# One more attention head in the seven-product form, a closer timetable, and moved buffers in a fused decoder layer

## The chip, the cores and the metric

The kernel runs on one core of a Trainium2 chip. The metric is the device time of one execution in microseconds (us), as the median of several runs. The core's engines work side by side, each through its own instruction queue in order: PE (TensorE, matrix products), DVE (VectorE), ACT (ScalarE), POOL (GpSimd) and SP (which here only issues transfers). PEld is PE's loading of weights. Matrix products are collected in PSUM, eight banks of 128 x 512 float32.

## The reference

One decoder layer on 512 tokens of width 2048 in float32. The part that the change is in is the token mixer:

```
h = rmsnorm(x, attn_pre_norm)
proj = h @ w_in                       # 2048 x 6160
gq, gk, gv, gg, ga, dq, dk, dv = ...  # column ranges of proj
...
o_a = gla_chunked(gq, gk, gv, log_a)                 # 4 heads, 128 keys, 256 values
o_a = rmsnorm(o_a, gla_norm) * silu(gg)
o_b = diff_attention(dq, dk, dv, lam)                # 4 heads, two softmaxes each
o_b = rmsnorm(o_b, diff_norm) * (1.0 - lambda_init)
m = concat(o_a, o_b) @ w_o
x = x + rmsnorm(m, attn_post_norm)
```

A gated MLP of width 5632 with a causal convolution follows; the change does not touch it.

## The kernel before

Every float32 operand of a large product is split into a high and a low part (`whi`, `wlo` for weights by `granule`, L116; `ah`, `al` for the activations), and a product is three matmuls: high by high, high by low, low by high. Weights come in granules of 128 x 1024 numbers (512 KB): ACT makes the high part, DVE the low one.

The stages are these. `first_half` loads x, normalizes and transposes it into `ah` and `al`, and begins the first 512 columns of gv. Set-up work stands behind it in the code (L474 to L530): masks, `keep`, the lambda sums, the columns of the convolution. Then the rest of gv, the forget gate's input (`forget_in`, with the small operand `gas`), and the sums for the next form (`mixer_sums`: `s5`, `s2`, `s3`).

Next come the units. A `Unit` (L209) computes 512 columns as two blocks of 256 with seven products of half size in place of eight (Strassen's scheme): fourteen granules, each 24 matmuls of 128x256 (`up_prods`, L318 to L320, or `token_prods`, L329 to L331). Sums of weight blocks are made by DMAs with addition on the POOL queue (`more`, L228) and by DVE. Units stand for gq and gk (two), the second half of gv, dv (two), and the first STRASSEN_HEADS heads of dq and dk. Their results go to DRAM and come back as rows when the attention wants them. `p1` (in `mix_unit.copy`) is a copy of the first product that a unit keeps until its last one.

The attention stage runs on a timetable. `gran` is a list of plain granules, each 24 matmuls of 128x512, in four parts; a part and what the timetable lays beside it make a tick. In the list stand dq and dk of the heads that are not units (`plan_t`, L162 to L164), the two halves of the gate gg (`plan_n`, L181 to L183, with `gate` at the end of each bank), and seven granules of w_o. `END` is the tick at which w_o begins. `spawn(gen, at)` puts a generator on tick `at`; each `yield n` sends it n ticks on. GLA_EVERY is the distance of the levels of a GLA head (`gla_head`, seven `gla_level`, `gla_tail`), BLOCK_EVERY that of the 16 `query_block`s, STATE_EVERY that of the four chunks in a `gla_tail`. `gated_row` multiplies GLA rows with gate rows and transposes them, `reload` brings a head of the differential attention back. Inside this stage the order on PE, ACT, DVE and POOL is that of the code; what waits, waits in its queue, and all behind it too. The attention's products take their PSUM banks from a ring of four (`psa`), the plain granules from another of four (`psm`).

The activation's lower left quarter is overwritten during the units and comes back from DRAM on the POOL queue in front of the last `y2`; the plain granules start with the half that was not overwritten.

Of the kernel before, what the change touches and what calls it, by code (L numbers as in the profile page):

```python
# [9 lines left out]
F32 = mybir.dt.float32  # L10
# [3 lines left out]
ALU = mybir.AluOpType  # L14
# [3 lines left out]
P = 128  # L18
D = 2048
S = 512  # L20
# [3 lines left out]
GH, GDK, GDV, RANK = 4, 128, 256, 16  # L24
TAU = 16.0
DH, DQK, DDV = 4, 128, 256
# [3 lines left out]
C_GQ, C_GK, C_GV, C_GG, C_GA, C_DQ, C_DK, C_DV = 0, 512, 1024, 2048, 3072, 3088, 4112, 5136  # L30
GR = 1024
LEVELS = [64, 32, 16, 8, 4, 2, 1]
STRASSEN_HEADS = 3
GLA_EVERY, BLOCK_EVERY, STATE_EVERY = 2.45, 6.2, 3


@with_exitstack
def hybrid_layer(ctx: ExitStack, tc: tile.TileContext, x, attn_pre_norm, w_in, w_alpha_up, b_alpha,
# [10 lines left out]
    def dma(o, i):  # L49
        return nc.sync.dma_start(out=o, in_=i)  # L50
# [7 lines left out]
    tt = nc.vector.tensor_tensor  # L58
# [247 lines left out]
    def up_room(pool):  # L306
        for n in ("s5", "s2", "s3"):
            up[n] = tuple(pool.tile([P, 2, HK, P], F32R, name=f"{n}{v}", bufs=1) for v in "hl")
# [159 lines left out]
    sums = ExitStack()  # L468
    early = ExitStack()
    so = early.enter_context(tc.tile_pool(name="so", bufs=1, side="right", reuse_waits="tile"))  # L470
    room["rt"] = rq = sums.enter_context(tc.tile_pool(name="rq", bufs=4, reuse_waits="tile"))
    mb = sums.enter_context(tc.tile_pool(name="mb", bufs=2, reuse_waits="tile"))
    up_room(so)
    so.tile([P, 120], F32, name="pad", bufs=1)  # L474

    def pair_tile(name="u"):
        return mb.tile([P, 2, S], F32, name=name, tag="u", bufs=4)
# [17 lines left out]
    gnb = mx1.tile([P, GDV], F32, name="gnb")  # L495
    bcast_row(gnb, gla_norm[0])
    dnb = mx1.tile([P, DDV], F32, name="dnb")
# [129 lines left out]
    def mix_unit(cols2, dsts, prods, store=dma):  # L627
        st = {}
        T = [slice(0, 256), slice(256, 512)]
        by_token = prods is token_prods  # L630

        def block(i, j, g):
            return w_in3[:, HK * i + 4 * g:HK * i + 4 * g + 4, cols2[j]:cols2[j] + 256]

        def tile_of(j):
            if j not in st:
                st[j] = pair_tile()
                if by_token:
                    st[j] = st[j].rearrange("p n (t e) -> p (n t) e", e=256)
            return st[j]  # L640

        def quad(half, j):
            return tile_of(j)[:, 2 * half:2 * half + 2, :] if by_token else tile_of(j)[:, :, T[half]]

        def copy():
            return mb.tile([P, 2, 256], F32, name="p1", tag="p1", bufs=2)

        def done(j):
            store(dsts[j], st[j])

        return Unit(4, block, prods, seven, quarters(quad, copy, done))
# [4 lines left out]
    units += [mix_unit((C_DQ + 256 * h, C_DK + 256 * h), (dqd[h], dkd[h]), up_prods,  # L656
                       dma_aside if h == STRASSEN_HEADS - 1 else dma) for h in range(STRASSEN_HEADS)]
    units[0].ahead()
# [17 lines left out]
    def gla_load(h):  # L676
        return [row("gr", v[h // 2][:, h % 2, :]) for v in (gqd, gkd, bd)]
# [6 lines left out]
    for i, u in enumerate(units):  # L684
# [6 lines left out]
        if nxt is None:  # L691
            early.close()
            ga = mixer.enter_context(tc.tile_pool(name="ga", bufs=2, side="right", reuse_waits="tile"))
# [25 lines left out]
    mc = mixer.enter_context(tc.tile_pool(name="mc", bufs=2, reuse_waits="tile"))  # L719
# [13 lines left out]
    def tg(name):  # L733
        return mc.tile([P, S], F32, name=name, tag="tg", bufs=4)
# [45 lines left out]
    def gla_tail(h):  # L780
        q, k, b = gla_in[h]
        bc = b.rearrange("p (c x) -> p c x", c=4)
        eb, sc = ebs[h], scs[h]
        vt = ga.tile([P, NT, GDV], F32, name="gv", tag="gv", bufs=1)
        dma(vt, gvd[h])
        kd = tg("kd")
        tt(kd.rearrange("p (c x) -> p c x", c=4), bc[:, :, P - 1:P].to_broadcast([P, 4, P]), bc, ALU.subtract)
        yield 1
        act(kd, kd, AF.Exp, scale=1.0 / TAU)
        yield 1  # L790
        tt(kd, kd, k, ALU.mult)
        qb = ga.tile([P, S], F32, name="qb", tag="qb", bufs=1)
        stt(qb, q, SG, eb, ALU.mult, ALU.mult)
        if h + 2 < GH:
            gla_in[h + 2] = gla_load(h + 2)
        yield 2
        kb = bank()
        for c in range(3):
            nc.tensor.transpose(kb[:, c * P:(c + 1) * P], kd[:, c * P:(c + 1) * P], ident)
        yield 1  # L800
        kT = mc.tile([P, S], F32, name="kT", tag="kT", bufs=1)
        act(kT[:, :3 * P], kb[:, :3 * P], AF.Copy)
        yield 2
        e0 = (h % 2) * GDV
        st, last = None, None
        for c in range(5):
            if last is not None:
                go, r = last
                act(go, go, AF.Copy, scale=r)
                dma(god[h // 2][:, c - 1, e0:e0 + GDV], go)  # L810
            if c == 4:
                break
            vc = vt[:, c, :]
            po = bank()
            if c:
                mm(po[:, :GDV], qb[:, c * P:(c + 1) * P], st, start=True, stop=False)
            mm(po[:, :GDV], sc[:, c, :], vc, start=c == 0, stop=True)
            if c < 3:
                pk = bank()
                mm(pk[:, :GDV], kT[:, c * P:(c + 1) * P], vc, start=True, stop=True)  # L820
            yield 1
            if c < 3:
                ns = mc.tile([P, GDV], F32, name="st", tag="st", bufs=2)
                if c == 0:
                    nc.vector.tensor_copy(ns, pk[:, :GDV])
                else:
                    stt(ns, st, eb[:, c * P + P - 1:c * P + P], pk[:, :GDV], ALU.mult, ALU.add)
                st = ns
            ss = small.tile([P, 1], F32, name="ss", tag="ss")
            act(po[:, GDV:], po[:, :GDV], AF.Square, accum_out=ss)  # L830
            go = mc.tile([P, GDV], F32, name="go", tag="go", bufs=2)
            tt(go, po[:, :GDV], gnb, ALU.mult)
            last = go, rsqrt_mean(ss, GDV)
            yield STATE_EVERY - 1

    def query_block(h, qb):
# [47 lines left out]
        p, p1 = ps[0][0], ps[1][0]  # L884
# [10 lines left out]
        po = bank()  # L895
        for j in range(qb + 1):
            mm(po[:, :DDV], aT[:, j * P:(j + 1) * P], vs[h][:, j, :], start=j == 0, stop=j == qb)
        yield 1
        ss = small.tile([P, 1], F32, name="ss", tag="ss")
        act(po[:, DDV:], po[:, :DDV], AF.Square, accum_out=ss)  # L900
        on = mc.tile([P, DDV], F32, name="on", tag="on", bufs=2)
        tt(on, po[:, :DDV], dnb, ALU.mult)
        r = rsqrt_mean(ss, DDV)
        yield 2
        act(on, on, AF.Copy, scale=r)
# [43 lines left out]
        yield 1  # L949

    def gate(c, t, b):
        sg = ga.tile([P, S], F32, name="sg", tag="sg", bufs=3)
        act(sg, b, AF.Sigmoid)
        yield 1
        tt(sg, sg, b, ALU.mult)  # L955
        dma(sgd[c][:, t, :], sg)
# [33 lines left out]
    order = [(s + 8) % 16 for s in range(KT)]  # L990
    for h in range(STRASSEN_HEADS, DH):
        plan_t(C_DQ + 256 * h, dqd[h], (2, 3, 0, 1) if h == STRASSEN_HEADS else (0, 1, 2, 3))
        plan_t(C_DK + 256 * h, dkd[h], (0, 1, 2, 3))
# [181 lines left out]
    sums = ExitStack()  # L1175
# [388 lines left out]
```

## Time and profile before

| | us |
|---|---|
| median of 3 runs | 2130.56 |
| lowest and highest run | 2129.01, 2130.93 |
| profiled execution, its time | 2129.44 |
| its span, first to last instruction | 2127.7 |
| start, up to the units | 0 to 81 |
| units | 81 to 403 |
| attention with plain granules | 403 to 664 |
| w_o and the MLP | 664 to 2128 |

The profile is of one execution. Rows of engine busy time give, for each stretch: its length, then for each engine the busy time and the number of instructions, then the granted PE clock as a share of full speed, the share in which the DMA engines were busy, and GB/s. Rows of groups give line, engine, operation, names and shape, count, busy time and mean ns, and after the last bar the idle time before them with what ended it. Rows of waits read "engine, line, waited for: total us, times, longest". Timeline rows give start, length, the instruction, and in brackets the idle time before it. SPq and POOLq are the queues that issue transfers.

### The profile page before, as it was taken

Reading aid. Unit: us, or ns where it says so; the run is one execution under the profiler, and the core shown is the slowest. Engines: PE = TensorE matmul, PEld = TensorE weight load, DVE = VectorE, ACT = ScalarE, POOL = GpSimd, SP = SyncE. Lnnn points to the kernel's source line nnn. Section 1 sums busy time; section 2 is a strip of 40 time slices with the busy share of each in tenths; the row PEclk is TensorE's granted clock in tenths of the full one; section 3 lists DMA queues with packets and bytes.
Section 4 is the critical chain, followed back from the end, with each engine's and each line's share of the span. In section 5 each row is a group of like instructions: output and inputs, shape, how many; then the busy total and the mean of one; then the engine's idle time right before and its main releaser. Section 6 shows DMA issues by size and latency. Waiting matters only on the chain.

```text
span 2127.7 us, 34806 instructions
## 1 busy us (share of the span) xinstructions
PE 2078.3 (98%) x14161; PEld 1898.2 (89%) x14161; DVE 1554.1 (73%) x1873; ACT 967.9 (45%) x1247; POOL 248.0 (12%) x281
## 2 busy tenths in 40 slices
PE   7899999999999999999999999999999999999997
PEld 6699999988878888899999999999999788788886
DVE  5967666577764246787787787877778777888887
ACT  4445344344553234344554544444454554444433
POOL 1111111011110000011101111011110110110101
PEclk9999999999999999999999999999999999999999
DMA  9267576844446344366757667577576877675753
GB/s 317 54 179 183 136 176 150 268 136 128 153 132 215 104 135 168 129 129 145 172 150 187 156 142 190 145 167 180 140 168 159 252 207 179 177 202 156 186 151 138
DMA packets 255269, 353.31 MB, mean 166 GB/s; under 512 B 14128, under 2 KB 185572, under 8 KB 253316
## 3 DMA queue, kind: packets, MB, share of 16 engines
q1 hardware_dynamic: 184260, 268.24, 37.1%
q0 software_dynamic: 70848, 82.85, 24.8%
q8 instruction: 111, 1.82, 0.3%
q14 instruction: 50, 0.41, 0.1%
HBM read 303.33 MB, written 47.71 MB: 165 GB/s over the span
## 4 chain that ended last, share of the span: by engine, by line
issue 30%; PE 23%; DMA 3%; DVE 2%; POOL 2%; ACT 0%; POOLq 0%; DVEq 0%; SPq 0%; ACTq 0%
PE bank L320 7%; PE bank L318 7%; PE bank L319 7%; POOL rt L228 1%; POOL raw L228 1%; DMA rt<-in_w_ffn_out_dram 1%; DMA raw<-in_w_ffn_in_dram 1%; DVE wlo L126 1%; PE bank L1469 0%; PE bank L1470 0%; DMA raw<-in_w_ffn_out_dram 0%; PE bank L1468 0%; DVE u L1502 0%; PE bank L164 0%; PE bank L163 0%
## 5 line engine op out<-in xcount | busy, mean ns | idle before, releaser
L125 ACT ACTIVATE whi<-raw 128x1024 fp32r<-128x1024 f32 x283 | 298.7, 1060 | 503.9 <-PE bank L319 168.4
L126 DVE TENSOR_TENSOR wlo<-raw,whi 128x1024 fp32r<-128x1024 f32 x283 | 343.8, 1221 | 228.2 <-ACT whi L125 225.9
L125 ACT ACTIVATE whi<-rt 128x1024 fp32r<-128x1024 f32 x306 | 322.8, 1060 | 364.7 <-PE bank L319 197.9
L126 DVE TENSOR_TENSOR wlo<-rt,whi 128x1024 fp32r<-128x1024 f32 x306 | 373.2, 1221 | 144.6 <-ACT whi L125 141.1
L320 PE MATMUL bank<-ah,wlo 128*128 128x256 f32 x1600 | 442.5, 277 | 0.8 <-DVE wlo L126 0.7
L318 PE MATMUL bank<-ah,whi 128*128 128x256 f32 x1600 | 442.1, 276 | 0.9 <-DVE u L352 0.9
L319 PE MATMUL bank<-al,whi 128*128 128x256 f32 x1600 | 442.0, 276 | 0.0
L320 PEld LDWEIGHTS bank<-ah,wlo 128*128 128x128 f32 x1600 | 300.4, 188 | 1.7 <-DVE wlo L126 1.7
L318 PEld LDWEIGHTS bank<-ah,whi 128*128 128x128 f32 x1600 | 300.4, 188 | 1.4 <-issue 1.0
L319 PEld LDWEIGHTS bank<-al,whi 128*128 128x128 f32 x1600 | 300.3, 188 | 0.1
L1345 PE MATMUL bank<-wlo,ah 128*128 128x512 f32 x560 | 219.4, 392 | 1.8 <-DVE wlo L126 1.5
L1344 PE MATMUL bank<-whi,ah 128*128 128x512 f32 x560 | 213.7, 391 | 6.8 <-DVE acc L1352 3.2
L1346 PE MATMUL bank<-whi,al 128*128 128x512 f32 x560 | 218.6, 391 | 0.0
L181 PE MATMUL bank<-whi,ah 128*128 128x512 f32 x448 | 185.4, 416 | 4.7 <-DVE sg L955 4.7
L182 PE MATMUL bank<-wlo,ah 128*128 128x512 f32 x448 | 176.1, 394 | 0.6 <-DVE wlo L126 0.5
L183 PE MATMUL bank<-whi,al 128*128 128x512 f32 x448 | 175.6, 394 | 0.0
L1344 PEld LDWEIGHTS bank<-whi,ah 128*128 128x128 f32 x560 | 105.2, 188 | 31.4 <-ACT whi L125 6.2
L1345 PEld LDWEIGHTS bank<-wlo,ah 128*128 128x128 f32 x560 | 105.6, 189 | 26.1 <-DVE wlo L126 4.3
L1346 PEld LDWEIGHTS bank<-whi,al 128*128 128x128 f32 x560 | 105.6, 188 | 21.9
L320 PE MATMUL bank<-s2h,wlo 128*128 128x256 f32 x400 | 111.5, 279 | 2.7 <-DVE wlo L126 2.7
L318 PE MATMUL bank<-s5h,whi 128*128 128x256 f32 x400 | 110.6, 277 | 1.0 <-ACT whi L125 1.0
L318 PE MATMUL bank<-s2h,whi 128*128 128x256 f32 x400 | 111.2, 278 | 0.0
(283 smaller groups left out, 4416.6 us busy)
## 6 DMA issues: line engine op xcount, KB each, us to landing
raw<-in_w_ffn_in_dram SPq DMA_DIRECT2D x96, 512.0 KB, 5.1
raw<-in_w_in_dram SPq DMA_DIRECT2D x64, 512.0 KB, 4.9
raw<-in_w_ffn_out_dram SPq DMA_DIRECT2D x48, 512.0 KB, 5.9
rt<-in_w_ffn_in_dram SPq DMA_DIRECT2D x40, 512.0 KB, 5.5
rt<-in_w_ffn_in_dram POOLq DMA_DIRECT2D x40, 512.0 KB, 5.9
raw<-in_w_ffn_in_dram POOLq DMA_DIRECT2D x40, 512.0 KB, 7.3
raw<-in_w_o_dram SPq DMA_DIRECT2D x32, 512.0 KB, 3.9
rt<-in_w_ffn_out_dram SPq DMA_DIRECT2D x20, 512.0 KB, 8.4
```

The lines of the kernel that those rows point to most:

```text
L125: act(hi, raw, AF.Copy)
L126: tt(lo, raw, hi.bitcast(F32), ALU.subtract)
L181: mm(banks[t], ah[:, t, s, :], w[0][:, k, :], start=st, stop=False)
L182: mm(banks[t], ah[:, t, s, :], w[1][:, k, :], start=False, stop=False)
L183: mm(banks[t], al[:, t, s, :], w[0][:, k, :], start=False, stop=sp)
L228: nc.gpsimd.dma_start(out=raws[g].rearrange("p (a b) -> p a b", a=self.a), in_=self.block(0, j, g), accum_op=ALU.add)
L318: mm(o, wh, sh[:, :, kk, :], start=start and kk == 0 and n == 0, stop=False, **NOW)
L319: mm(o, wh, sl[:, :, kk, :], start=False, stop=False, **NOW)
L320: mm(o, wl, sh[:, :, kk, :], start=False, stop=kk == HK - 1, **NOW)
L1344: mm(b[j], sh[:, o:o + P], w[0][:, q, :], start=start and st == 0, stop=False, **NOW)
L1345: mm(b[j], sh[:, o:o + P], w[1][:, q, :], start=False, stop=False, **NOW)
L1346: mm(b[j], sl[:, o:o + P], w[0][:, q, :], start=False, stop=st == 3, **NOW)
```

## The change

STRASSEN_HEADS goes from 3 to 4: dq and dk of the last head, eight granules at the head of the plain list, become one more unit. `gran` then has 16 granules before w_o instead of 24, so END is tick 64 instead of 96, and the timetable's three distances shrink. `p1` gets a pool of its own. In `gla_tail` and `query_block` the DVE product with the norm's gain stands in front of ACT's square of the same PSUM bank. Gate rows of the second half take tiles of the ring `gr` (six deep, of GLA's own rows), and the last of the first half one of `ro`, so that the three-deep ring `sg` is not asked for them.

```
-STRASSEN_HEADS = 3
-GLA_EVERY, BLOCK_EVERY, STATE_EVERY = 2.45, 6.2, 3
+STRASSEN_HEADS = 4
+GLA_EVERY, BLOCK_EVERY, STATE_EVERY = 1.7, 4.3, 2
...
     mb = sums.enter_context(tc.tile_pool(name="mb", bufs=2, reuse_waits="tile"))
+    mp = sums.enter_context(tc.tile_pool(name="mp", bufs=2, reuse_waits="tile"))
...
         def copy():
-            return mb.tile([P, 2, 256], F32, name="p1", tag="p1", bufs=2)
+            return mp.tile([P, 2, 256], F32, name="p1", tag="p1", bufs=2)
...
+            go = mc.tile([P, GDV], F32, name="go", tag="go", bufs=2)
+            tt(go, po[:, :GDV], gnb, ALU.mult)
             ss = small.tile([P, 1], F32, name="ss", tag="ss")
             act(po[:, GDV:], po[:, :GDV], AF.Square, accum_out=ss)
-            go = mc.tile([P, GDV], F32, name="go", tag="go", bufs=2)
-            tt(go, po[:, :GDV], gnb, ALU.mult)
...
+        on = mc.tile([P, DDV], F32, name="on", tag="on", bufs=2)
+        tt(on, po[:, :DDV], dnb, ALU.mult)
         ss = small.tile([P, 1], F32, name="ss", tag="ss")
         act(po[:, DDV:], po[:, :DDV], AF.Square, accum_out=ss)
-        on = mc.tile([P, DDV], F32, name="on", tag="on", bufs=2)
-        tt(on, po[:, :DDV], dnb, ALU.mult)
...
     def gate(c, t, b):
-        sg = ga.tile([P, S], F32, name="sg", tag="sg", bufs=3)
+        sg = mc.tile([P, S], F32, name="sg", tag="ro", bufs=2) if (c, t) == (0, 3) else (
+            ga.tile([P, S], F32, name="sg", tag="gr", bufs=6) if c else ga.tile([P, S], F32, name="sg", tag="sg", bufs=3))
         act(sg, b, AF.Sigmoid)
```

Lines behind the pool `mp` stand one further down than before and those behind the gate's tile two: a block's scores, L846, are L847 now, and the gate's sigmoid, L953, is L955, which before was its product on DVE (now L957).

Outside the timetable a scheduler sets the order, and it moves the set-up work at the start. On DVE, before, this is what stands behind the last transposed quarter of x (`al` of L139); `setup` holds the masks in the making, `q` is a sum for the units:

```order
L139 TENSOR_TENSOR al<-bank,ah 128x512 x2
L487 MEMSET setup 128x64 x7
L493 MEMSET keep 128x512
L613 TENSOR_TENSOR q<-ah 128x1024 x2
L494 MEMSET keep 128x4
L490 CAST masks<-setup 128x256
L614 TENSOR_TENSOR q<-q,al 128x1024
L506 TENSOR_TENSOR setup<-setup 128x256
```

And on DVE at the beginning of the program, now:

```order
L73 MEMSET nhalf 128x4
L488 MEMSET setup 128x64 x7
L494 MEMSET keep 128x512
L495 MEMSET keep 128x4
L491 CAST masks<-setup 128x256 x7
L409 SCALAR_TENSOR_TENSOR xt<-xt,rs,gb 128x512 x2
L126 TENSOR_TENSOR wlo<-raw,whi 128x1024
```

The masks went in front of the first scale of x (L409), and behind the last `al` there now follow `q`, `gas` and the splits at once.

In the attention the program sets the order itself. On PE, before, where the second head's query blocks begin (`dr` are the rows of q and k of a query block, `qe` and `d` a GLA level, `s` the weights of a block under transposition, L162 to L164 the plain matmuls of a tick):

```order
L846 MATMUL bank<-dr 128x128
L774 MATMUL bank<-qe,d 128x64 x4
L890 MATMUL bank<-ident,s 128x128 x4
L162 MATMUL bank<-ah,whi 128x512
L163 MATMUL bank<-al,whi 128x512
L164 MATMUL bank<-ah,wlo 128x512
```

The same place now (`gv` with `sc` and `kT` is a chunk of a GLA tail, `dv` with `aT` the output of a block):

```order
L847 MATMUL bank<-dr 128x128
L818 MATMUL bank<-gv,sc 128x256
L821 MATMUL bank<-gv,kT 128x256
L898 MATMUL bank<-dv,aT 128x256 x3
L775 MATMUL bank<-qe,d 128x64 x4
L181 MATMUL bank<-whi,ah 128x512
L182 MATMUL bank<-wlo,ah 128x512
L183 MATMUL bank<-whi,al 128x512
```

The first five rows now fall into one tick and take five banks; before, three rows stood in such a tick.

On ACT at the second half of the gate, before (`sg` is a gate row by the sigmoid, L860 the exponentials, which need another table):

```order
L953 ACT_TABLE_LOAD
L953 ACTIVATE sg<-bank 128x512
L809 ACTIVATE go<-go,rs 128x256
L953 ACTIVATE sg<-bank 128x512
L900 ACTIVATE bank,ss<-bank 128x256
L953 ACTIVATE sg<-bank 128x512
L931 ACTIVATE ah<-bank 128x512
L830 ACTIVATE bank,ss<-bank 128x256
L1025 ACTIVATE whi<-raw 128x1024
L905 ACTIVATE on<-on,rs 128x256
L953 ACTIVATE sg<-bank 128x512
```

And now:

```order
L955 ACT_TABLE_LOAD
L955 ACTIVATE sg<-bank 128x512 x2
L894 ACTIVATE aT<-bank 128x128
L861 ACT_TABLE_LOAD
L861 ACTIVATE s,l<-s,nm 128x256
L906 ACTIVATE on<-on,rs 128x256
L955 ACT_TABLE_LOAD
L955 ACTIVATE sg<-bank 128x512
L932 ACTIVATE ah<-bank 128x512
L833 ACTIVATE bank,ss<-bank 128x256
L1027 ACTIVATE whi<-raw 128x1024
L955 ACTIVATE sg<-bank 128x512
```

An exponential now stands between the gate rows, with a table load on either side of it.

## The prediction

> **What bounds the kernel now.** The page comes first: span, busy time by engine, and the slices.
>
> ```profile
> span 2127.7 us, 34806 instructions
> PE 2078.3 (98%) x14161; PEld 1898.2 (89%) x14161; DVE 1554.1 (73%) x1873; ACT 967.9 (45%) x1247; POOL 248.0 (12%) x281
> PE   7899999999999999999999999999999999999997
> DVE  5967666577764246787787787877778777888887
> ```
>
> TensorE (PE) is busy nearly everywhere, so the kernel gets shorter only by less matmul time or by removing the few places where PE waits. Slice 1 (53 to 106 us) is one: PE 8, VectorE (DVE) 9. The profiled execution took 2129.44 us, 1.7 us more than its span; the median of the runs is 2130.56 us, 1.1 us above it. I work out a difference against the profiled execution and apply it to the median.
>
> Next, busy time by stretches: one unit of the seven-product form, a stretch of plain products alone, the whole attention stage, its dense middle, and the slice in it where DVE is busiest.
>
> ```profile
> core 0: us, PE busy (x) PEld busy (x) DVE busy (x) ACT busy (x) POOL busy (x), PEclk, DMA share, GB/s
> 332.46:370.54 38.08, 38.08 (x339) 38.08 (x338) 25.14 (x24) 15.87 (x16) 5.13 (x4) 1.00 0.62 139
> 680.00:760.00 80.00, 80.00 (x354) 66.27 (x353) 21.75 (x20) 19.47 (x27) 0.00 (x0) 1.00 0.34 106
> 403.00:664.00 261.00, 255.89 (x1306) 212.51 (x1306) 184.77 (x437) 131.58 (x295) 26.57 (x65) 1.00 0.48 154
> 430.00:610.00 180.00, 179.26 (x929) 149.99 (x928) 134.57 (x335) 93.80 (x219) 21.29 (x52) 1.00 0.43 137
> 550.00:580.00 30.00, 29.40 (x146) 24.00 (x146) 24.01 (x61) 16.82 (x39) 3.82 (x10) 1.00 0.53 163
> ```
>
> The first stretch runs from the first s5 product of one unit to that of the next: a unit of 336 matmuls of 128x256 costs 38.08 us, 0.1133 us each. Plain products run at 80/354 = 0.226 us for a 128x512, so a granule of 24 takes 5.42 us and a plain pair of eight granules 43.4 us. In the dense middle DVE is busy 134.57/180 = 75%, and PE hardly waits.
>
> The waits of PE itself are asked for in the two stages that the change touches, first the attention, then the start.
>
> ```profile
> PE bank L181 <- DVE sg L955: 4.7, 3, 3.0
> PE bank L774 <- DVE rl L865: 0.5, 1, 0.5
> ...
> PE bank L320 <- DVE wlo L126: 3.4, 3, 2.7
> PE bank L557 <- DVE gas L139: 2.3, 1, 2.3
> PE bank L318 <- ACT whi L125: 1.0, 1, 1.0
> ```
>
> In the attention PE loses 5.2 us, nearly all at the gates; at the start 6.7 us, every time for a split that stands late in a queue.
>
> **The pair that changes its form.** Eight plain granules go (-43.4) and one unit comes (+38.1): **-5.3 us**, both bound by PE. Its first row of busy times says that a unit keeps DVE busy 25.1 of 38.1 us and ScalarE (ACT) 15.9, so its 14 splits, its additions and its four accumulating transfers on the POOL queue stay hidden, as in the five units before it; without that cover its DVE work is 25.1 us. Four held-row copies on ACT and their stores go too; nothing waited for them.
>
> The unit loads weights for every 256 columns, the plain pair for every 512. A load takes 0.188 us by its group's row, more than the 0.1133 us between two matmuls, and yet PE and its loads are busy for the same 38.08 us: they overlap.
>
> ```profile
> L318 PEld LDWEIGHTS bank<-ah,whi 128*128 128x128 f32 x1600 | 300.4, 188 | 1.4 <-issue 1.0
> ```
>
> [...]
>
> **The start.** In the new order 21 small DVE instructions (masks, keep, wup, the lambda sums) stand at the front of the queue or among the norm's scales instead of among the first splits, and gas is split earlier. These are the larger groups, and what the two longer waits did to PE's clock:
>
> ```profile
> L490 DVE CAST masks<-setup 128x256 uint8<-128x256 f32 x7 | 2.8, 425 | 0.7 <-POOL setup L489 0.7
> L487 DVE MEMSET setup<- 128x64 f32 x7 | 0.6, 112 | 0.0
> L493 DVE MEMSET keep<- 128x512 f32 x1 | 0.5, 485 | 0.1
> L550 DVE MEMSET wup<- 48x512 f32 x1 | 0.5, 485 | 0.0
> ```
>
> ```profile
> 72.00:75.00 3.00, 3.00 (x8) 1.38 (x7) 3.00 (x4) 0.52 (x2) 0.00 (x0) 0.50 0.97 235
> 100.00:106.00 6.00, 3.46 (x16) 3.47 (x17) 6.00 (x7) 2.00 (x2) 0.00 (x0) 0.72 0.01 3
> ```
>
> These four groups alone take 4.4 us off a queue that is busy without a gap while PE waits (3.00 of 3.00, 6.00 of 6.00), more than the longest single wait, 2.7 us. Each of the two longer waits was followed by matmuls at a granted clock of 0.50: eight at 0.43 instead of 0.23 us, 1.6 us lost, and about as much by estimate in the second row. So 6.7 + 3.2 = 9.9 us can be had.
>
> Against it stand the work that moved to POOL's front, 14 selects ahead of the first root mean square, and eight small loads that SP's queue now issues ahead of the next weights.
>
> ```profile
> 8.39 1.41 DVE L409 SCALAR_TENSOR_TENSOR xt<-xt,rs,gb 128x512 f32<-128x512 f32 x2 [7.46 <-POOL rs L134]
> ...
> 1.83 0.60 POOL L481 TENSOR_SCALAR_AFFINE_SELECT dist<-dist 128x512 f32<-128x512 f32 x1
> 7.24 0.19 POOL L404 TENSOR_TENSOR ss<-ss 128x1 f32<-128x1 f32 x1 [4.81 <-ACT jb L402]
> ...
> 55.91 0.24 POOL L489 TENSOR_SCALAR_AFFINE_SELECT setup<-setup 128x64 f32<-128x64 f32 x1
> 56.10 1.10 POOL L488 TENSOR_SCALAR_AFFINE_SELECT setup<-setup 128x64 f32<-128x64 f32 x2
> ...
> 49.15 0.43 SPq L50 DMA_DIRECT2D setup<-in_lambda_k_dram  x1
> ```
>
> POOL is free for 4.8 us before it is needed. A select took 0.24 us while DVE stood still and 0.55 with DVE running, so 14 take 3.4 to 7.7 us: the first scale moves by 0 to 3 us. The eight loads delay the weights by 8 x 0.43 = 3.4 us, beside that delay rather than on top of it. Ends for the start: -9.9 and +3. I take **-7**, near the first end, since PE's waits there are for the very queue that is relieved.
>
> **Gates and order in the attention.** These rows carry it: DVE's wait behind ACT's square, ACT's wait for an old gate row's store, and in order of time the two events beneath PE's longest wait and a table load.
>
> ```profile
> DVE on L902 <- ACT bank L900: 27.6, 14, 3.5
> ...
> ACT sg L953 <- DMA sgd<-sg: 8.6, 2, 6.4
> ```
>
> ```profile
> 627.30 0.60 ACT L953 ACTIVATE sg<-bank 128x512 f32<-128x512 f32 x1 [6.36 <-DMA sgd<-sg]
> ...
> 628.81 0.42 DVE L832 TENSOR_TENSOR go<-bank,gnb 128x256 f32<-128x256 f32 x1 [4.83 <-ACT bank L830]
> ...
> 634.22 1.28 ACT L860 ACT_TABLE_LOAD   x1
> ```
>
> ACT waited 6.36 us for a buffer of the three-deep gate ring, the square of L830 stood behind it, DVE's product stood behind the square, and the gate's own product, for which PE waits, came last. Now the product goes first and the second gate half takes rows of another ring, so this chain is cut twice. What comes instead: ACT's square waits for DVE's product, and behind it on ACT stand the next exponential, a weight split or a gate; the weight split feeds PE, three ticks ahead. The product takes 0.42 us. At the second gate half ACT loads its table four times instead of twice, 2.6 us at the 1.28 us of such a load, and DVE is denser. So PE keeps some wait here: between 0 and 8 us against 5.2 now. I take 3: **-2**, ends -5.2 and +3.
>
> **The closer timetable.** All attention work now falls on 64 + 28 ticks instead of 96 + 28 (a tick is a quarter of a granule). The intervals shrink by 2.45/1.7 = 1.44 and 6.2/4.3 = 1.44. The dense 180 us hold 19 granules, as this row, which counts their DVE splits, shows:
>
> ```profile
> 430.00:610.00 180.00, 23.16 (x19) 1.00 0.43 137
> ```
>
> Of PE's 179.3 us, 19 x 5.42 = 103 are plain and 76 attention; of DVE's 134.6, 23.2 are splits and 111.4 attention. The same attention work now lies beside 19/1.44 = 13.2 granules: PE 71.5 + 76 = 147.5 us, DVE 111.4 + 16.1 = 127.5, or 86% instead of 75%. PE stays the longer engine, but not by much, and PSUM gets tight: five attention products can fall into one tick, four banks hold them, and PE then waits until DVE has emptied the first. Does a DVE at 86% stall PE? Rows for both answers:
>
> ```profile
> 60.00:104.00 44.00, 37.49 (x223) 29.47 (x223) 40.97 (x45) 19.47 (x27) 3.49 (x4) 0.94 0.28 62
> 880.00:920.00 40.00, 40.00 (x219) 34.71 (x218) 36.56 (x36) 17.62 (x19) 2.64 (x2) 1.00 0.39 97
> 1870.00:1910.00 40.00, 40.00 (x178) 33.14 (x177) 35.93 (x40) 19.57 (x20) 5.48 (x6) 1.00 0.74 193
> ```
>
> At 91% and 90% PE lost nothing where its inputs were ready well ahead; at 93% with short leads it lost 6.5 of 44 us, 15%. On 147.5 us that is 0 to 22 us. The leads here are one to two ticks, between the two cases; I take **+6**, nearer the lower end, because the attention at up to 80% (24.01 of 30) lost PE time only at a gate.
>
> At the end the last block's rows are ready at tick 83 of 92 instead of 111 of 124. Nine ticks of 1.36 us are 12.2 us; they cover the store and the reload:
>
> ```profile
> dr<-dod SPq DMA_DIRECT2D x4, 256.0 KB, 3.0
> ...
> dod<-do SPq DMA_DIRECT2D x5, 128.0 KB, 4.4
> ```
>
> 4.4 + 3.0 = 7.4 us leave 4.8 for the splits behind them: I take nothing, and up to 7.4 if the blocks end that much later. Head 3's GLA rows are stored from tick 64 on and read back from tick 67 on, before from 88 and 99: three dense ticks of 147.5/52.8 = 2.8 us cover the store, and the product comes three ticks after the load: nothing.
>
> **Sum:** -5.3 - 7 - 2 + 6 = **-8.3 us**; 2129.44 becomes 2121.1 and the median 2130.56 becomes **2122.3 us**. What a measurement of this kernel can tell from no change is about 0.2%, 4.3 us.
>
> **Rivals.** *All clean:* no wait is left at start or gates and the denser ticks cost nothing: -5.3 - 9.9 - 5.2 = -20.4, 2110.2 us. For it: DVE at 90% elsewhere without loss. Against: four banks, short leads. Chance 0.14.
>
> *The gain does not show:* PE meets other late splits at the start, or small transfers push the weights back (0 instead of -7): -5.3 - 2 + 6 = -1.3, 2129.3 us; likewise if the dense ticks cost 12 instead of 6. For it: four engines feed the start and one wait gives way to the next. Against: DVE's queue there is really shorter. Chance 0.26.
>
> *Slower, the bank ring:* with DVE at 86% the four PSUM banks turn over faster than DVE empties them, and each oversubscribed tick stops PE, as at the start: 15% of 147.5 us is 22, and -5.3 - 7 - 2 + 22 = +7.7, 2138.3 us. It makes the kernel slower by over 0.2% once these waits pass 5.3 + 7 + 2 + 4.3 = 18.6 us. For it: 1.44 times the products per tick through the same ring, and granted clock falls after a long wait. Against: the ring never cost more than 0.5 us at 75%, at a granted clock of 1.00. Chance 0.19. [...]
>
> *Loads in series:* if the new unit's weight loads did not lie beside its matmuls, they would add 336 x 0.188 = 63 us, and -8.3 + 63 = +54.7 gives 2185.3 us. Five units of the same shape speak against it; chance below 0.01. [...]
>
> **The numbers.** My forecast has 0.40. Faster by over 0.2%: 0.40 + 0.14 = 0.54; within 0.2%: 0.26; slower: 0.20. The range reaches from 2113 us, just short of all clean, to 2137, short of the full price of the bank ring; the forecast's own range is 2117 to 2126.
>
> **What would show it.** The unit at 38.1 us; PE without waits for L557 and s2's wlo and the clock at 1.00 from 60 to 106 us; no wait of ACT for sgd; an attention stage near 220 us with DVE at about 80% over it, and PE's waits there near 9 us in all, on DVE's exits from PSUM (L779, L828, L851) and the gates. Waits of PE above 18 us there, or a start as long as before, would make the prediction wrong.

## The result and the profile after

The changed kernel takes **2114.95 us** (median of 4 runs, 2110.82 to 2115.63) beside 2129.78 us of the kernel before in the same comparison: a ratio of 0.9928, 95% interval 0.9911 to 0.9945, or 14.8 us less. The profiled execution took 2115.09 us, its span is 2113.4 us where it was 2127.7.

From the page of the changed kernel: span, busy time, and the slices of PE.

```profile
span 2113.4 us, 35113 instructions
PE 2069.1 (98%) x14305; PEld 1895.9 (90%) x14305; DVE 1568.2 (74%) x1888; ACT 973.6 (46%) x1253; POOL 253.5 (12%) x285
PE   7999999999999999999999999999999999999997
```

The 8 in slice 1 of PE is a 9 now. PE's share is 98% as before: it was the bound and still is, so all of the gain is work or waiting taken from PE. Where, the stretches say: one unit, the attention stage, its dense middle, and the 44 us at the start in which PE lost 6.5 us before.

```profile
321.02:359.03 38.01, 38.01 (x337) 38.01 (x337) 24.55 (x23) 15.86 (x16) 5.13 (x4) 1.00 0.70 167
431.00:653.00 222.00, 217.74 (x1123) 179.97 (x1122) 174.94 (x430) 123.30 (x286) 30.08 (x65) 0.99 0.47 157
450.00:600.00 150.00, 148.05 (x789) 123.65 (x788) 130.07 (x336) 85.91 (x208) 22.30 (x48) 0.99 0.42 138
60.00:104.00 44.00, 42.97 (x302) 37.54 (x301) 43.28 (x41) 22.18 (x28) 2.55 (x2) 1.00 0.41 101
```

A unit takes 38.0 us. The attention stage's 222 us hold about as many products (1123) as the 261 us before without the plain pair's 192 (1306 - 192 = 1114); DVE is busy 79% over the stage and 130.07/150 = 87% in the dense middle, where it was 75%. In the last row PE is busy 42.97 instead of 37.49 us, at a clock of 1.00 instead of 0.94.

What PE waited for at the start (60 to 125 us):

```profile
PE bank L318 <- ACT whi L125: 1.0, 1, 1.0
PE bank L320 <- DVE wlo L126: 0.2, 1, 0.2
```

The waits for `gas` (L557, 2.3 us) and nearly all of that for the low weight halves (3.4 us) are gone. And in the attention (425 to 650 us, with the end of the last unit, whose wait for `u` is the third row):

```profile
PE bank L910 <- ACT bank L903: 0.9, 1, 0.9
PE bank L821 <- DVE sc L779: 0.9, 1, 0.9
PE bank L318 <- DVE u L352: 0.9, 1, 0.9
PE bank L817 <- ACT bank L833: 0.8, 1, 0.8
PE bank L818 <- DVE s L851: 0.7, 1, 0.7
PE bank L847 <- ACT bank L833: 0.5, 1, 0.5
PE bank L847 <- DVE st L826: 0.2, 1, 0.2
PE bank L775 <- DVE s L851: 0.2, 1, 0.2
```

The long wait at the gate (4.7 us) is gone. In its place stand short ones, each for a PSUM bank of the ring of four that DVE or ACT has not emptied yet (`s`, `sc`, `st`, the squares of L833 and L903).

Three marks in PE's own record, the same in all kernels, divide the span: the first product of the second unit (its first with `s5h`), the last product of the last unit, and the first transposition of the MLP's input (L146). "Attention" below is the time from the second mark to the third, w_o's granules included. "Waits" are PE's idle gaps over 0.1 us in it. "Lost to the clock" is the share of the clock that was not granted, times the stretch in which it was missing: 8 x (1 - 0.79) = 1.7 us for the changed kernel at 520 to 528 us, and the same for the pool alone at 615 to 623 us.

| us | before | after | pool alone | pool undone | three units' heads |
|---|---|---|---|---|---|
| second unit begins | 132.0 | 121.5 | 121.4 | 132.2 | 121.3 |
| last unit ends | 404.5 | 431.0 | 393.0 | 442.3 | 393.3 |
| attention | 388.2 | 346.0 | 390.5 | 343.8 | 383.0 |
| its waits | 5.7 | 5.0 | 6.4 | 4.6 | 1.3 |
| lost to the clock in it | 0 | 1.7 | 1.7 | 0 | 0 |
| the rest | 1335.1 | 1336.4 | 1331.9 | 1334.4 | 1337.5 |

Before to after: the units end 26.5 us later with one unit of 38.0 us more, so the start gave 11.5 us; the attention gave 42.2; the rest, which the change does not touch, took 1.3 more (it lies between 1331.9 and 1340.0 us over all the kernels here). 38.0 - 11.5 - 42.2 + 1.3 = -14.4 us, against -14.3 in the spans. Each mark is from one execution, and the attention of three kernels with the same attention code differs by 2.7 us (388.2, 390.5, and 390.9 below), so differences under 2 us are not read. Most of that scatter is the clock: these three lost 0, 1.7 and 3.4 us to it (the last with 0.72 over 615 to 627 us), and without that they took 388.2, 388.8 and 387.5 us.

### The profile page after: what moved, and what is told of

It reads as the page before. It is cut to its first block, busy times and chain, and to the rows that moved or that the text cites. A ratio compares the mean times of both kernels' runs of the same rounds, so it can differ in the third digit from the quotient of the medians.

```text
span 2113.4 us, 35113 instructions
## 1 busy us (share of the span) xinstructions
PE 2069.1 (98%) x14305; PEld 1895.9 (90%) x14305; DVE 1568.2 (74%) x1888; ACT 973.6 (46%) x1253; POOL 253.5 (12%) x285
## 4 chain that ended last, share of the span: by engine, by line
issue 35%; PE 13%; DMA 4%; DVE 4%; POOL 3%; ACT 1%; POOLq 0%; DVEq 0%; SPq 0%; ACTq 0%
PE bank L1347 3%; PE bank L1348 3%; PE bank L1346 3%; POOL rt L228 1%; DVE wlo L126 1%; POOL raw L228 1%; DMA rt<-in_w_ffn_in_dram 1%; DMA raw<-in_w_ffn_in_dram 1%; DMA rt<-in_w_ffn_out_dram 1%; PE bank L320 1%; PE bank L319 1%; PE bank L318 1%; ACT whi L125 0%; PE bank L1471 0%; PE bank L1472 0%
## 5 line engine op out<-in xcount | busy, mean ns | idle before, releaser
L126 DVE TENSOR_TENSOR wlo<-raw,whi 128x1024 fp32r<-128x1024 f32 x289 | 351.0, 1221 | 241.3 <-ACT whi L125 240.8
L125 ACT ACTIVATE whi<-rt 128x1024 fp32r<-128x1024 f32 x314 | 330.6, 1059 | 362.7 <-PE bank L319 191.7
L126 DVE TENSOR_TENSOR wlo<-rt,whi 128x1024 fp32r<-128x1024 f32 x314 | 383.0, 1221 | 145.1 <-ACT whi L125 144.7
L320 PE MATMUL bank<-ah,wlo 128*128 128x256 f32 x1664 | 460.4, 277 | 0.7 <-DVE wlo L126 0.5
L318 PE MATMUL bank<-ah,whi 128*128 128x256 f32 x1664 | 459.9, 276 | 0.9 <-DVE u L352 0.9
L319 PE MATMUL bank<-al,whi 128*128 128x256 f32 x1664 | 459.7, 276 | 0.0
L320 PEld LDWEIGHTS bank<-ah,wlo 128*128 128x128 f32 x1664 | 312.3, 188 | 1.8 <-DVE wlo L126 1.7
L318 PEld LDWEIGHTS bank<-ah,whi 128*128 128x128 f32 x1664 | 312.4, 188 | 1.4 <-issue 1.0
L319 PEld LDWEIGHTS bank<-al,whi 128*128 128x128 f32 x1664 | 312.3, 188 | 0.1
L320 PE MATMUL bank<-s5h,wlo 128*128 128x256 f32 x416 | 115.0, 276 | 0.2 <-DVE wlo L126 0.2
```

The costliest lines, as they stand in the source:

```text
L125: act(hi, raw, AF.Copy)
L126: tt(lo, raw, hi.bitcast(F32), ALU.subtract)
L318: mm(o, wh, sh[:, :, kk, :], start=start and kk == 0 and n == 0, stop=False, **NOW)
L319: mm(o, wh, sl[:, :, kk, :], start=False, stop=False, **NOW)
L320: mm(o, wl, sh[:, :, kk, :], start=False, stop=kk == HK - 1, **NOW)
```

## The experiments

**The pool.** The kernel before with only `p1` moved out of `mb`, and the changed kernel with only that undone.

```
+    mp = sums.enter_context(tc.tile_pool(name="mp", bufs=2, reuse_waits="tile"))
...
-            return mb.tile([P, 2, 256], F32, name="p1", tag="p1", bufs=2)
+            return mp.tile([P, 2, 256], F32, name="p1", tag="p1", bufs=2)
```

Expected of the first:

> The kernel before with one edit: p1 in a pool of its own. Theory (room): the start alone gains what the trace of the changed kernel shows there, 10.5 us at the second unit, plus about 1 us by the last unit, so 2118 to 2120 us; the attention stage keeps its 261 us and its 5.2 us of PE waits. Rival (the start's gain needs the other edits, or is given back where the units meet the attention): 2128 to 2131 us, within 2 us of before.

Measured: 2118.83 us, ratio 0.9947 [0.993, 0.9964], which is 11.3 us of 2130.64. From 60 to 104 us it reads as the changed kernel does (PE 42.97 us, DVE 43.28, clock 1.00):

```profile
60.00:104.00 44.00, 42.97 (x303) 37.55 (x302) 43.28 (x41) 22.21 (x28) 2.55 (x2) 1.00 0.41 101
```

Expected of the second:

> The changed kernel with p1 back in the pool mb. Theory (room): the start loses its 10.5 us again, so 2125 to 2127 us, and the attention stage is as long as in the changed kernel. Rival (the gain lies in the pair, the gates and the timetable, and the pool only moves a wait): 2114 to 2117 us.

Measured: 2123.71 us, ratio 0.9966 [0.9955, 0.9978]. The old waits of PE at the start are back:

```profile
PE bank L320 <- DVE wlo L126: 4.3, 5, 2.6
PE bank L557 <- DVE gas L139: 2.3, 1, 2.3
```

The units end at 442.3 instead of 431.0 us, so the start loses 11.3 us. The time is still 1.3 us under the expected range: the attention took 343.8 us, 2.2 less than in the changed kernel, and 1.7 of these are the clock, which comes back below.

So the start is the pool's, whatever stands in the attention. But why does a pool for a copy that units make move masks at the program's beginning? In the built program `mb` with `p1` reached up to 179200 in a partition and so lay over one of the norm's x tiles (175616 to 183808); without `p1` it ends at 175104. What is made in `mb` then no longer has to follow the norm. If that is so, any other 4 KB taken out of `mb` will do. The next kernel is the one before with `p1` left where it was, and the three set-up tiles of the tag `qs` moved instead:

```
-        gar = mb.tile([P, S], F32, name="gar", tag="qs", bufs=2)
+        gar = mp.tile([P, S], F32, name="gar", tag="qs", bufs=2)
...
-        wup = mb.tile([P, S], F32, name="wup", tag="qs", bufs=2)[:48, :]
+        wup = mp.tile([P, S], F32, name="wup", tag="qs", bufs=2)[:48, :]
...
-        gaT = mb.tile([P, S], F32, name="gaT", tag="qs", bufs=2)[:48, :]
+        gaT = mp.tile([P, S], F32, name="gaT", tag="qs", bufs=2)[:48, :]
```

> The kernel before with p1 left in its pool, and the three short-lived set-up tiles gar, wup and gaT (512 columns of float32 each, a ring of two) taken out of it instead. My theory: what the pool's split did at the start was only to make the pool mb shorter, so that it no longer lies over the address of one of the norm's x tiles and the set-up work behind it may go first; p1 itself has no part in it. Then this kernel does as the pool alone did: 2118 to 2121 us, the first unit near 83 us and the second near 121. The rival: p1's own ring mattered (the units' copies waited for tiles shared with it): no change, 2128 to 2131 us, the first unit near 87.5 us and the second near 132.

Measured: 2121.52 us, ratio 0.9954 [0.9941, 0.9968]; the second unit begins at 122.3 us, the attention takes 390.9.

```profile
60.00:104.00 44.00, 42.97 (x303) 37.56 (x302) 42.79 (x40) 22.18 (x28) 2.55 (x2) 1.00 0.39 95
```

The time is half a microsecond past the range; the first unit begins at 82.7 us (82.8 with the pool alone), the second within 1 us of it, and the row is nearly the same. `p1` has no part in it; the length of `mb` has. In this program `gar` and `wup` themselves lie over that x tile (175104 to 179200), and the waits do not come back. One thing is argued and not run: both kernels also have one pool more than before, and it is the addresses that speak for the length and not for the further pool.

**The fourth unit and the density.** The changed kernel with the plain pair and the old timetable, so with pool, ring and order alone:

```
-STRASSEN_HEADS = 4
-GLA_EVERY, BLOCK_EVERY, STATE_EVERY = 1.7, 4.3, 2
+STRASSEN_HEADS = 3
+GLA_EVERY, BLOCK_EVERY, STATE_EVERY = 2.45, 6.2, 3
```

> The changed kernel with three plain units beside the attention and the old timetable (one head less in the seven-product form); pool, gate tiles and order stay as changed. Theory (room, and a dense timetable that costs as much as the pair gives): start -11, gates -4 to -5 against before, no pair: 2113 to 2116 us, no more than 2 us from the changed kernel. Rival (the pair's 5.3 us come through whole): 2119 to 2121 us.

Measured: 2114.16 us, ratio 0.9913 [0.9894, 0.9932]: the time of the changed kernel, whose ratio is 0.9928 [0.9911, 0.9945]. Its attention has one wait of PE in the list, and its dense middle none:

```profile
PE bank L775 <- DVE rl L866: 0.5, 1, 0.5
```

```profile
420.00:600.00 180.00, 180.00 (x933) 150.80 (x933) 136.73 (x334) 94.00 (x221) 24.50 (x52) 1.00 0.45 138
```

With DVE at 136.73/180 = 76% PE is busy 180.00 of 180.00 us. So the mends of ring and order gave 388.2 - 383.0 = 5.2 us, and from here to the changed kernel 383.0 - 43.4 = 339.6 became 346.0: the density cost 6.4 us in this execution, more than the pair's 5.3. Of the 6.4, 1.7 are the clock; by the changed kernel with the pool undone, in which it did not fall, the density cost 343.8 - 339.6 = 4.2 us.

Next, the closer timetable with the plain pair kept, which separates the density from what the fourth unit itself brings (`STRASSEN_HEADS = 3`, the rest as changed):

> The changed kernel with three units' heads and the plain pair back, but the closer timetable kept: the attention work lies as dense as in the changed kernel, and plain granules run alone behind it, before the second half of the gate. If the density is what costs, the attention takes 4 to 7 us more than with the wider timetable and the same heads (383.0 us): 387 to 390 us, and 2118 to 2121 us. The rival: the 6.4 us belong to what the fourth unit brings (its rows through DRAM, another place of the gate's halves), not to the density: 383 to 385 us, and 2113.5 to 2116 us.

Measured: 2116.14 us, ratio 0.9928 [0.9914, 0.9941], attention 386.4 us, 3.4 more than with the wider timetable, waits 4.0 instead of 1.3. What PE waited for:

```profile
PE bank L891 <- ACT bank L903: 1.2, 1, 1.2
PE bank L775 <- DVE d L771: 1.1, 1, 1.1
PE bank L910 <- DVE s L851: 0.6, 1, 0.6
...
```

Both expectations missed, between them: the closer timetable alone brings waits for banks of the same kind, but 3.4 of the 6.4 us. The clock, below, makes up 1.7 of the other 3.0, and beside the 4.2 us without a fall of the clock the 3.4 are the same within the scatter.

**The order of square and product.** The changed kernel with the two lines put back in `gla_tail` and `query_block`:

```
-            tt(go, po[:, :GDV], gnb, ALU.mult)
             ss = small.tile([P, 1], F32, name="ss", tag="ss")
             act(po[:, GDV:], po[:, :GDV], AF.Square, accum_out=ss)
+            tt(go, po[:, :GDV], gnb, ALU.mult)
...
```

> The changed kernel with ACT's square of a block and of a GLA chunk ahead of DVE's product again. Theory (DVE at 86% has little idle time to spend on waits behind ACT): the waits of the product for the square come back, some 25 us on DVE in a stage of 220 us, and 3 to 8 us of them reach PE: 2118 to 2123 us. Rival (DVE's slack takes them): 2114 to 2117 us.

Measured: 2114.91 us, ratio 0.9924 [0.9907, 0.994], attention 346.4 us. My theory of a dearer old order falls: at this density the swap is worth nothing that shows. It moved a wait from one engine to the other. Before, DVE waited 27.6 us for ACT (`on` L902); in the changed kernel ACT waits for DVE's product:

```profile
ACT bank L903 <- DVE on L901: 31.2, 14, 4.4
ACT bank L833 <- DVE go L831: 15.6, 12, 3.9
```

Of these waits 2.2 us reach PE by its own list above (0.9, 0.8 and 0.5); with the old order its waits in the attention are 5.7 us, with the new one 5.0.

**The gate's ring.** The changed kernel with all gate rows in the three-deep ring again:

```
-        sg = mc.tile([P, S], F32, name="sg", tag="ro", bufs=2) if (c, t) == (0, 3) else (
-            ga.tile([P, S], F32, name="sg", tag="gr", bufs=6) if c else ga.tile([P, S], F32, name="sg", tag="sg", bufs=3))
+        sg = ga.tile([P, S], F32, name="sg", tag="sg", bufs=3)
```

> The changed kernel with one mend undone: all eight gate rows again take the three-deep ring sg. My theory: this ring, and not the order of square and product, cost PE its waits at the gates, so ScalarE again waits for the store of an old gate row (sgd) ahead of a sigmoid, the gate's product comes late, and PE waits 3 to 5 us for it: 2118 to 2121 us where the changed kernel has about 2115, with PE's waits in the attention at 8 to 10 us instead of 5.0. The rival: with the closer timetable the rows are stored and free early enough anyway, ScalarE does not wait for sgd, and the time stays within 1 us of the changed kernel.

Measured: 2118.09 us, ratio 0.9938 [0.9925, 0.9951], attention 350.0 us, 4.0 more, with waits of 7.6 instead of the 8 to 10 expected. The interval overlaps the changed kernel's, so the total alone does not prove it; the trace has the chain. ACT in order of time (start, length, instruction, idle before it):

```profile
513.72 1.28 ACT L954 ACT_TABLE_LOAD   x1 [3.10 <-DMA sgd<-sg]
515.01 0.60 ACT L954 ACTIVATE sg<-bank 128x512 f32<-128x512 f32 x1
```

DVE behind it:

```profile
515.64 0.69 DVE L956 TENSOR_TENSOR sg<-sg,bank 128x512 f32<-128x512 f32 x1 [2.06 <-ACT sg L954]
517.94 0.16 DVE L866 RECIPROCAL rl<-l 128x1 f32<-128x1 f32 x1 [1.61 <-ACT s L861]
...
521.33 0.68 DVE L851 SCALAR_TENSOR_TENSOR s<-dist,bank 128x512 f32<-128x512 f32 x1
```

and the longest wait of PE in that stage:

```profile
PE bank L818 <- DVE s L851: 2.4, 1, 2.4
```

ACT stands 3.1 us for the store of an old gate row, the exponential and the operations behind it come late, and DVE, which stands for them in turn, empties the scores' bank so late that PE waits 2.4 us for it instead of 0.7. Of the 4.0 us, 2.6 are waits; the rest is the clock, which stayed low for longer (0.66 over 520 to 530 us, so 3.4 us lost instead of 1.7). The theory holds in kind: the wait reaches PE by way of DVE's queue, not by the gate's own product.

**What the density costs.** First DVE's load. The softmax goes without its maximum, which leaves out 64 DVE instructions and the protection against large scores that it gives:

```
-            mxv = small.tile([P, 1], F32, name="mxv", tag="mxv")
-            nc.vector.reduce_max(mxv, s[:, :nk], axis=AX.X)
-            nm = small.tile([P, 1], F32, name="nm", tag="nm")
-            ts(nm, mxv, -SC, None, ALU.mult)
...
-            act(s[:, :nk], s[:, :nk], AF.Exp, bias=nm, scale=SC, accum_out=l)
+            act(s[:, :nk], s[:, :nk], AF.Exp, scale=SC, accum_out=l)
```

> The changed kernel without the softmax's maximum: reduce_max over the scores and its scaling are left out, and the exponential has no bias (which leaves the softmax the same in exact arithmetic). It takes 64 DVE instructions, some 20 us, out of the dense stage and leaves PE's work alone. If a busy DVE is what costs the dense stage its 6.4 us, 4 to 6 of them go: 2109 to 2111 us. The rival: PE waits there because a bank of the ring of four is asked for again too soon after its products (by the distance of the ticks' products, whatever the load), and the maxima are not in its way: at most 2 us go, 2113 to 2115 us.

Measured: 2111.74 us, ratio 0.9907 [0.9894, 0.9921]; attention 342.4, waits 3.0. That is 3.6 us off the attention, between the two expectations and nearer to the load. The dense middle and the 8 us in which the changed kernel's clock fell:

```profile
450.00:600.00 150.00, 149.13 (x805) 125.19 (x804) 116.76 (x289) 85.35 (x210) 22.13 (x48) 1.00 0.44 138
...
520.00:528.00 8.00, 7.28 (x35) 5.29 (x34) 6.35 (x16) 5.63 (x15) 1.48 (x4) 1.00 0.62 215
```

Here is the same stretch in the changed kernel, and what stood in front of it on PE:

```profile
520.00:528.00 8.00, 7.18 (x27) 5.14 (x28) 6.03 (x15) 5.93 (x15) 1.48 (x4) 0.79 0.73 228
```

```profile
519.04 0.70 PE L818 MATMUL bank<-gv,sc 128*128 128x256 f32 x2 [0.71 <-DVE s L851]
520.62 0.70 PE L821 MATMUL bank<-gv,kT 128*128 128x256 f32 x2 [0.89 <-DVE sc L779]
...
521.84 2.01 PE L847 MATMUL bank<-dr 128*128 128x512 f32 x2 [0.19 <-DVE st L826]
```

Three waits for banks within 4 us, none above 0.9, and the granted clock falls: 0.79 over 8 us, which is 8 x 0.21 = 1.7 us. Here five attention products (L910, L818, L821, L891, L847) stand between two plain ones and want four banks. Without the maxima DVE is at 116.76/150 = 78%, the wait for `sc` goes and the clock stays at 1.00: 2.0 us of waits and 1.7 of clock make the 3.6 us.

The clock's part, though, cannot be put down to the maxima. In the changed kernel with the pool undone this place comes 10.9 us later, the same three products (one line higher there) wait just as long, and the clock stays at 1.00:

```profile
529.92 0.70 PE L817 MATMUL bank<-gv,sc 128*128 128x256 f32 x2 [0.72 <-DVE s L850]
531.51 0.70 PE L820 MATMUL bank<-gv,kT 128*128 128x256 f32 x2 [0.89 <-DVE sc L778]
...
532.73 1.13 PE L846 MATMUL bank<-dr 128*128 128x512 f32 x2 [0.19 <-DVE st L825]
```

```profile
531.00:539.00 8.00, 7.30 (x35) 5.77 (x36) 6.46 (x17) 5.82 (x15) 1.49 (x4) 1.00 0.72 236
```

Its attention took 343.8 us with waits of 4.6. Beside that the kernel without the maxima gained 1.4 us, all of it in waits, which is what its rival allowed ("at most 2 us"). So DVE's load is shown as the cause of a part of the waits only; the total does not settle it either, since its interval overlaps the changed kernel's.

The clock fell at this one place (0.79 behind waits of 0.71, 0.89 and 0.19 us), behind waits none of which was as long as 1 us, and not as a rule: the same three waits with the pool undone left it at 1.00, and in the dense stage's other cluster, from 604 to 611 us, with waits of 0.79, 0.91 and 0.46 us, it stayed at 1.00 as well.

Then the ring. `pk` takes the free half of the bank of `po`, so that a chunk asks the ring for one bank less; the square is written over its own input:

```
-                pk = bank()
-                mm(pk[:, :GDV], kT[:, c * P:(c + 1) * P], vc, start=True, stop=True)
+                pk = po[:, GDV:]
+                mm(pk, kT[:, c * P:(c + 1) * P], vc, start=True, stop=True)
...
-            act(po[:, GDV:], po[:, :GDV], AF.Square, accum_out=ss)
+            act(po[:, :GDV], po[:, :GDV], AF.Square, accum_out=ss)
```

> The changed kernel with one product fewer per chunk in the ring of four PSUM banks: the state's product (pk) takes the unused second half of the output's bank (po), and the square is written over its own input, which the gain has read by then. DVE's work stays as it is. If the dense stage's 6.4 us come from banks that are asked for again too soon, 3 to 6 of them go: an attention of 340 to 343 us instead of 346.0, PE's waits there under 2.5 us instead of 5.0, 2109 to 2112 us. If they come from DVE's load, the queue of DVE is as late as before and at most 1.5 go: 2113.5 to 2115 us.

Measured: 2113.88 us, ratio 0.9916 [0.9902, 0.993], attention 343.5, but waits 4.7 us where under 2.5 were expected of it.

```profile
PE bank L847 <- ACT bank L833: 0.9, 1, 0.9
...
PE bank L891 <- ACT bank L903: 0.7, 1, 0.7
PE bank L817 <- ACT bank L833: 0.7, 1, 0.7
PE bank L818 <- DVE s L851: 0.7, 1, 0.7
...
PE bank L891 <- DVE sc L779: 0.5, 1, 0.5
```

The waits only stand elsewhere: where `pk` waited, the next product (L891) now does, for the same `sc` in DVE's queue. The clock stays at 1.00, but so it did with the pool undone and the bank not shared; beside that kernel's 343.8 us the attention is only 0.3 shorter. So no gain can be put down to the ring. The theory that a bank is asked for too soon fails as it was put; the time is that of its rival.

Both reliefs together, no maximum and the shared bank:

> Both reliefs at once: the shared bank, and no softmax maximum (left out as in the run without it). If load and ring are two sides of one thing (a bank that DVE empties too late for the next product), nearly all of the 6.4 us go: attention 339.5 to 341 us, PE's waits there under 1.5 us, 2108 to 2110 us, the fastest of all these kernels. If the loss lies elsewhere, in PE's own order or its clock, it stays where the run without the maximum was, with an attention near 342.4 us and 2110.5 to 2112 us.

Measured: 2108.14 us, ratio 0.9894 [0.9877, 0.991]; attention 341.6, waits 3.0. The median is the lowest of all kernels here and within the 2108 to 2110 expected; the interval ends just below where the changed kernel's begins (0.9911), so this version is faster than the changed kernel by the least that the intervals can tell. The attention lies just past the expected 341, and the waits are not under 1.5: they are those of the run without the maximum, so for the waits the rival was right and the ring added nothing that can be told from the 2 us scatter.

Last, a timetable in which fewer products fall together (`BLOCK_EVERY` 4.0 instead of 4.3):

> The changed kernel with BLOCK_EVERY at 4.0 instead of 4.3: the query blocks stand closer, DVE is busier by about 7% of its share of them, but fewer products of other chains fall into the same tick, so that a bank of the ring is asked for again less soon after its last use. If the time is lost by which products meet in a tick, it is 1 to 3 us faster than the changed kernel, 2112 to 2114 us, with PE's waits in the attention under 4 us. If it is lost by DVE's load, it is 1 to 4 us slower, 2116 to 2119 us, with waits of 6 us or more.

Measured: 2114.04 us, ratio 0.9915 [0.99, 0.993], attention 345.8, waits 5.6. The time lies just past the first range and the waits between the two, so neither theory is borne out; one wait went and another came:

```profile
PE bank L891 <- ACT bank L903: 3.0, 2, 2.5
PE bank L775 <- DVE sc L779: 1.2, 2, 1.1
```

## Why the prediction was right in kind and short in size

It forecast -8.3 us and named the mechanism; -14.8 came, inside its range of 2113 to 2137 us and below the 2117 to 2126 of the forecast itself. By its own terms:

- **The pair, -5.3: held.** The unit took 38.01 us (38.08 forecast). Its weight loads lay beside its matmuls again (38.01 and 38.01 in its row), so the loads in series did not occur.
- **The start, -7 between -9.9 and +3: the term that was mis-sized.** It was -11.5 by the profile and -11.3 by the run of the pool alone. The mechanism was as put: small set-up work off DVE's queue, waits for `gas` and `s2` gone, clock at 1.00. The discount of 3 us for work that moves to POOL and SP was wrong: the 14 selects took 4.65 us and the first scale of x came 0.2 us later, at 8.60 instead of 8.39.

```profile
1.83 2.21 POOL L489 TENSOR_SCALAR_AFFINE_SELECT setup<-setup 128x64 f32<-128x64 f32 x7
...
4.58 2.44 POOL L490 TENSOR_SCALAR_AFFINE_SELECT setup<-setup 128x64 f32<-128x64 f32 x7
7.45 0.19 POOL L404 TENSOR_TENSOR ss<-ss 128x1 f32<-128x1 f32 x1 [0.42 <-ACT jb L402]
```

They filled the 4.8 us that POOL had stood idle, with 0.42 to spare. On SP's queue nine small loads stand ahead of the next weights, which go out from 25.84 us on instead of 16.71; that is 9 us where 3.4 had been put, and still PE idled only 0.5 us more in the first 60 us (11.5 instead of 11.0). The clean end of -9.9 was too small as well: of the 11.5 us, 4.6 came by the first unit (82.9 instead of 87.5), 5.9 more by the second and 1.0 by the last. Waits went from 9.6 to 4.0 us over the part up to the units' end, 5.6 us, and the two stretches at a reduced clock were worth about 3.4 (by the granted 0.83 over 70 to 80 and again over 100 to 110 us). The other 2.5 us were not traced further.
- **Gates and order, -2 between -5.2 and +3: mis-sized.** With the wider timetable it was -5.2, the clean end: of the 3 us left for ACT's waits and its table loads, none reached PE there. What did it was the ring (4.0 us when undone at the new density, 1.7 of them clock); the order, which the prediction gave a share, has none that shows. At the closer timetable the waits that the 3 us stood for did come. The second half of the gate has four table loads, as forecast; ACT's square comes late behind one of them and a gate row, or waits for DVE's product, and PE waits for the bank:

```profile
602.40 1.28 ACT L955 ACT_TABLE_LOAD   x1
603.69 0.60 ACT L955 ACTIVATE sg<-bank 128x512 f32<-128x512 f32 x1
...
604.67 0.39 ACT L833 ACTIVATE bank<-bank 128x256 f32<-128x256 f32 x1
...
605.22 0.70 PE L817 MATMUL bank<-st,qb 128*128 128x256 f32 x2 [0.79 <-ACT bank L833]
```

With the two waits behind it (0.91 and 0.46) that is 2.2 us. They stand in the next term's 6.4; put down to the gates, this term is -3.0 and the next +4.2.
- **The closer timetable, +6 between 0 and 22: held, +6.4.** DVE went to 87% in the dense middle (86% forecast) and 79% over the stage. The cost has three parts: 5.0 - 1.3 = 3.7 us of waits for banks, 1.7 of clock, and 1.0 that no view gave a cause for. The clock's part did not come with the pool undone, where the cost is 4.2. The price was carried over from a start with short leads; that it came so near was luck: +6 is the place between the rows that I chose, not something the rows gave.
- **The rivals.** All clean was right to take no discount at the start and the gates and wrong on the dense ticks: -5.3 - 9.9 - 5.2 with +6.4 is -14.0. The slower case, the bank ring, was there in kind, waits on just these exits, but at 3.7 us of waits where it put 22.
- **What would show it.** Waits of PE in the dense stage were expected near 9 us; they are 4.2 there, since the gates' own products have none. No wait of ACT for `sgd` is left.

Summed with the measured terms: -5.3 - 11.5 - 5.2 + 6.4 = -15.6 us, and the untouched rest's +1.3 makes -14.3.

The density cost 3.4 us with the plain pair kept and 6.4 with the fourth unit; without the fall of the clock it cost 3.4 and 4.2 (pool undone), which single executions do not tell apart. What stays open is why the clock fell in the one kernel and not in the other behind the same waits, the 2.5 us of the start, and the 1.0 of the density.

## What to carry to other kernels

Where the bounding engine waits for the very queue that a change relieves, and a row shows idle time that takes the moved work, count the whole wait and the clock lost behind it; here the 3 us taken off out of caution were the larger part of the error at the start. A cheaper form of a product that takes away what other work hid beside can give its gain back in density: here 4 to 6 us against 5.3, seen only when each was run without the other. When single executions are compared, take off what each lost to the clock first: here it hid that one bank less in the ring changed next to nothing. A set-up that stands late may wait for nothing but an address: a pool shorter by 4 KB in a partition was worth 11.3 us.

## What the runs showed of the hardware

The granted clock fell behind waits that were short, 0.79 over 8 us behind waits of 0.71, 0.89 and 0.19 us, and did not fall behind the same three with the pool undone. Each fall read here cost 1.7 us (0.79 over 8 us) or twice that (0.66 over 10 us). Some stand where no edit reaches: in the MLP the kernel before has 0.83 over 1690 to 1700 us, and the changed kernel 1.00 over 1670 to 1700. In the changed kernel with the pool undone, PE idled more between 60 and 104 us than in the kernel before (36.49 us busy, not 37.49), and yet the clock was at 1.00 there, where it was 0.94; it fell later:

```profile
60.00:104.00 44.00, 36.49 (x225) 28.92 (x225) 40.81 (x46) 19.48 (x27) 3.66 (x4) 1.00 0.28 62
94.00:112.00 18.00, 15.00 (x114) 14.60 (x114) 18.00 (x18) 7.19 (x8) 0.00 (x0) 0.91 0.22 62
```

So the length of the waits did not tell whether the clock would fall.
